# FoX: values stored by head, normalisation of a pair of heads within the next pair, GDN inverse tiles zeroed once by GpSimd; tail: sample work and SSD chunks spread among output-projection tiles

## The chip, the cores and the metric

The kernel runs on one core of a Trainium2 chip. The time is that of the device, in microseconds (us), from the first instruction to the last. Engines are named as in the profile: PE is TensorE (PEld its weight loads), DVE is VectorE, ACT is ScalarE, POOL is GpSimd, SP is SyncE, which only issues DMAs. A "q" behind the name (SPq) is the engine's sequencer, which also issues DMAs.

## The reference, cut to what matters

One layer of a hybrid model with four mixers of width 512 each, on a prompt of 1024 tokens and on 8 x 4 = 32 sample tokens. In the words of the reference:

```
proj  = x @ w_in
y_a   = rms_norm(gated_delta_rule(q, k, v, g, beta, S0)) * silu(a_gate)        # GDN, 4 heads
y_b   = rms_norm((ssd_scan(x, dt, A, B, C, h0) + D * x) * silu(b_gate)) * ssd_norm_w   # SSD, 8 heads, 2 groups
y_c   = forgetting_attention(q, k, v, cumsum(logf)) * silu(c_gate)             # FoX, 8 heads of 64
y_d   = softmax(q @ memory_k) @ memory_v * silu(d_gate)                        # memory attention
mixed = concat(y_a, y_b, y_c, y_d)                                             # 2048 wide
x_new = layer_norm(ALPHA * x + mixed @ w_out)
```

The samples have states and a paged cache of their own. Inputs and outputs are float32.

## The kernel before, in words

Work is laid out with features on the partitions. Large products run as three passes, high part times high part, high times low, low times high: `mh` is a tile rounded by ACT (L1545), `ml` is what is left of it (POOL, L1546), and the weights `wo` have both parts (ACT L1516, DVE L1517).

The stages of the profiled execution are: projections with the paged decode up to some 760 us; a change of memory pools up to 826; the **FoX stage** up to 1157; the **tail** up to 1374; the **last output group** to the end.

In the FoX stage `fox(hp)` (L545) runs four pairs of heads. For each head it loads queries and keys on the POOL queue and, once a pair, the values `vt` (L568, one buffer) and the gate `g2` on the SP queue; then for four pairs of query blocks it computes scores (`fs`, L588, with a minimum on DVE, L592), exponentials on ACT (L598), transposes (`ft`, copied to `P`) and products with the values (`fo`, L620), which DVE multiplies into `g2` (L626). After both heads it normalises: the reciprocal row sums are spread by ACT and transposed by PE (`fr`, by the helper in L219) and multiplied in by DVE (L640). Steps of `weave` alternate this with the GDN generator: `gdn_inv` (L1035) zeroes a tile `D1` (DVE, L1039) and loads diagonal blocks into it (L1041; POOL queue for the first half-head, SP for the others), `gdn_solve` inverts the chunk matrices (with `A` of L1057, masked in L1082), and `gdn_scan` runs over the chunks (`su`, `u`, L1160 to L1174). The last projections and the memory attention (`cross`) go on beside it.

In the tail, before: `out_w(12, 16)` loads weights of the output projection, two tiles of `mixed` are prepared ahead (`pre`), then in program order come the memory attention of the samples, `gdn_sample` (`xws`, `xM`), `ssd_sample` (`yi`, `yu`, `yo`), the eight SSD chunks (`ssd`, L1331) and the output groups 12 to 16, 8 to 12, 0 to 4, of eight tiles of 128 tokens each (`out`, L1549). In `out` a tile is two halves of 12 matmuls into `op` (L1574); `mixed` (L1540) loads `mr` on the SP queue (L1544) with two buffers. `out_s` gathers the 32 sample rows in `accs` (L1535). In an SSD chunk the decay `bE` is loaded, shifted and clipped by DVE (L1378, eight per chunk), exponentiated by ACT (L1380) and multiplied by `cb` on POOL (L1382); `bx` (L1350) holds the inputs, `Cz` (L1355, POOL) is a zero-padded copy of C by group, and `bb` (L1365) is the product B C. The last group, 4 to 8, is the SSD part; it starts with the sample rows (tile 8, L1576) and each tile ends with LayerNorm and its store (L1587 to L1603).

A planner (the tile framework) gives each engine its order: program order is the priority, an instruction goes when its inputs and its slot are expected ready, and `issue_after(x)` puts it behind instruction x of its engine. On the chip each engine and each DMA queue keeps that order. A tile with `bufs=n` waits for the last reader of the tile n before it.

## Time and profile before

| what | before |
| --- | --- |
| median of 3 runs (lowest, highest) | 1441.57 us (1438.98, 1443.81) |
| the profiled execution | 1434.86 us |
| its span in the trace | 1433.1 us |
| mean granted clock of TensorE | 0.976 |
| busy in the span: PE, DVE, ACT, POOL | 1329.7, 823.8, 494.7, 442.4 us |

A busy time is the sum of an engine's instructions; PEclk in a row is the granted clock as a share of full speed, 2.4 GHz, so that 0.5 is the lower of its two levels, 1.2 GHz. A wait is the idle time ahead of an instruction, with the operation whose end released it. A row `L620 ... fo<-P,vt` is the instruction at line 620, which writes `fo` from `P` and `vt`. The rows of waits have the time in all, the number of times and the longest.

### The profile page before, as it was taken

How to read it: one execution, taken by the hardware profiler on the slowest of the kernel's cores; microseconds unless marked ns; L12 is line 12 of the kernel's file. 1: busy time of each engine (PE TensorE's matmuls, PEld its weight loads, DVE VectorE, ACT ScalarE, POOL GpSimd, SP SyncE). 2: the span in 40 equal slices, each digit the busy share in tenths (PEclk: the TensorE clock that was granted, in tenths of full speed). 3: DMA queues.
4: the chain of work that ended last, by engine and by line, in shares of the span. 5: the costliest groups of instructions: out<-in, count | busy, mean ns of one | idle time of the engine just before them, and what ended most of it. 6: DMA issues, size and time to landing. Idle time of an engine off the chain costs nothing. (4 is left out here: it accounts for less than half of the span.)

```text
span 1433.1 us, 30270 instructions
## 1 busy us (share of the span) xinstructions
PE 1329.7 (93%) x11222; PEld 1110.0 (77%) x11222; DVE 823.8 (57%) x2141; ACT 494.7 (35%) x1280; POOL 442.4 (31%) x465
## 2 busy tenths in 40 slices
PE   7999999999899999999998899898988979999995
PEld 6899888888778877888887878776766756666764
DVE  4523223256576767534245655677676648856588
ACT  4422222233435343322233244454444421213232
POOL 1445322233425444432212100011111026544456
PEclk9999999999999999999999999899999999999998
DMA  6559888978778897888877834657547576655322
GB/s 246 196 169 374 331 299 323 321 269 281 240 284 306 282 307 248 303 287 323 308 259 175 239 91 118 239 147 208 137 129 252 175 234 205 198 160 121 96 67 106
DMA packets 184477, 324.30 MB, mean 226 GB/s; under 512 B 47177, under 2 KB 110954, under 8 KB 184330
## 3 DMA queue, kind: packets, MB, share of 16 engines
q1 hardware_dynamic: 113744, 241.39, 50.4%
q10 hardware_dynamic: 41930, 59.11, 11.6%
q0 software_dynamic: 28656, 21.88, 6.2%
q8 instruction: 88, 1.44, 0.4%
q14 instruction: 59, 0.48, 0.1%
HBM read 262.23 MB, written 60.01 MB: 225 GB/s over the span
## 5 line engine op out<-in xcount | busy, mean ns | idle before, releaser
L356 PE MATMUL pj<-xh,wh 128*128 128x352 f32 x1152 | 382.2, 333 | 13.1 <-ACT wh L341 5.0
L356 PE MATMUL pj<-xh,wl 128*128 128x352 f32 x1152 | 379.5, 329 | 3.3 <-DVE wl L342 3.3
L356 PE MATMUL pj<-xl,wh 128*128 128x352 f32 x1152 | 379.1, 329 | 0.0
L356 PEld LDWEIGHTS pj<-xh,wh 128*128 128x128 f32 x1152 | 219.1, 191 | 28.1 <-issue 10.7
L356 PEld LDWEIGHTS pj<-xh,wl 128*128 128x128 f32 x1152 | 219.8, 191 | 11.5 <-issue 6.3
L356 PEld LDWEIGHTS pj<-xl,wh 128*128 128x128 f32 x1152 | 219.3, 190 | 10.6 <-issue 9.9
L1574 PE MATMUL op<-wo,mh 128*128 128x512 f32 x512 | 162.9, 398 | 3.1 <-DVE lr L1587 1.6
L672 POOL DMA_INDIRECT lf<-in_logf,ix x64 | 67.9, 1062 | 203.4 <-DVE cb L675 163.4
L342 POOL TENSOR_TENSOR wl<-wr,wh 128x1024 fp32r<-128x1024 f32 x41 | 97.9, 2387 | 104.3 <-ACT wh L341 94.3
L742 DVE SCALAR_TENSOR_TENSOR Oacc<-Oacc,dmb,dO 128x512 f32<-128x512 f32 x64 | 47.5, 743 | 142.3 <-PE dO L737 134.1
L1574 PEld LDWEIGHTS op<-wo,mh 128*128 128x128 f32 x512 | 95.6, 190 | 29.6 <-issue 6.0
L1574 PE MATMUL op<-wo,ml 128*128 128x512 f32 x256 | 102.0, 401 | 5.5 <-POOL ml L1546 5.5
L917 DVE SCALAR_TENSOR_TENSOR y<-u,cw,y 128x1080 f32<-128x1080 f32 x54 | 80.1, 1484 | 21.9 <-ACT y L915 21.5
L718 PEld LDWEIGHTS dA<-pg,QD 128*32 128x32 f32 x2048 | 59.8, 109 | 39.7 <-issue 25.8
L718 PE MATMUL dA<-pg,QD 128*32 128x128 f32 x2048 | 80.6, 275 | 7.6 <-DMA pg<-in_cache 7.5
L598 ACT ACTIVATE S<-S,mn 128x512 f32<-128x512 f32 (+2 forms) x96 | 58.5, 610 | 50.8 <-DVE mn L592 24.3
L737 PE MATMUL dO<-pg,dP 128*32 128x512 f32 x512 | 71.8, 605 | 4.1 <-ACT dP L734 3.9
L726 ACT ACTIVATE dmb<-dmb 128x1 f32<-128x1 f32 x64 | 18.7, 293 | 131.6 <-DVE dmb L725 116.3
L1574 PEld LDWEIGHTS op<-wo,ml 128*128 128x128 f32 x256 | 48.4, 189 | 20.2 <-POOL ml L1546 7.1
L592 DVE CUSTOM_DVE_ANT_0 S<-fs,cB 128x512 f32<-128x512 f32 (+2 forms) x96 | 52.5, 551 | 19.9 <-PE ft L219 15.0
L1193 POOL TENSOR_TENSOR rb<-ra,constG 128x4 f32<-128x4 f32 (+1 forms) x9 | 8.7, 971 | 156.5 <-DVE ra L1192 156.5
L620 PE MATMUL fo<-P,vt 128*64 128x128 f32 x576 | 47.9, 288 | 9.6 <-DMA vt<-vD 7.7
(521 smaller groups left out, 2450.2 us busy)
## 6 DMA issues: line engine op xcount, KB each, us to landing
pg<-in_cache SPq DMA_DIRECT2D x256, 512.0 KB
wr<-in_w_in SPq DMA_DIRECT2D x48, 512.0 KB
k<-kD POOLq DMA_DIRECT2D x16, 512.0 KB, 18.2
wq<-in_w_out SPq DMA_DIRECT2D x16, 512.0 KB
mr<-mixD SPq DMA_DIRECT2D x32, 256.0 KB
xr<-in_xT SPq DMA_DIRECT2D x8, 528.0 KB
gateD<-gt ACTq DMA_DIRECT2D x24, 176.0 KB
mrow<-in_w_mem SPq DMA_DIRECT2D x8, 512.0 KB
```

The lines of the kernel that those rows point to most:

```text
L342: (eng or self.se).tensor_tensor(out=l, in0=r, in1=h.bitcast(F32), op=ALU.subtract)
L356: nc.tensor.matmul(ps[:n], lhsT=w[:, k, :], rhs=x[:, k, s], start=(k == 0 and q == 0), stop=(k == KD - 1 and q == 2))
L592: nc.vector.tensor_tensor_reduce(out=S[:, :w], in0=p[:, :w], in1=cB[:, c0:c1], op0=ALU.add, op1=ALU.min, scale=1.0, scalar=3e38, accum_out ...
L598: nc.scalar.activation(out=S[:, :w], in_=S[:, :w], func=AF.Exp, scale=-1.0, bias=mn[:, 0:1], accum_out=rs[:, qt, h2, i:i + 1])
L620: d = nc.tensor.matmul(o[64 * half:64 * half + 64, 0:128], lhsT=vt[:, kt, 64 * h2:64 * h2 + 64], rhs=P[qt, b4], start=(kt == 0), stop=(kt ...
L672: nc.gpsimd.indirect_dma_start(out=lf, out_offset=None, in_=I["logf"], in_offset=bass.IndirectOffsetOnAxis(ap=ix[:, j:j + 1].bitcast(U32), ...
L718: nc.tensor.matmul(ps[32 * b:32 * b + 32, 0:n], lhsT=QD[:, 4 * gr + b, hp, :], rhs=key(hp, b), start=(hp == 0), stop=(hp == 3), tile_posit ...
L726: nc.scalar.activation(out=mb[:, 1:2], in_=m, func=AF.Exp, scale=-1.0, bias=mb[:, 0:1])
L737: nc.tensor.matmul(po[32 * b:32 * b + 32, :], lhsT=P[:n, 32 * b:32 * b + 32], rhs=value(b), start=True, stop=True, tile_position=(0, 32 * b))
L742: nc.vector.scalar_tensor_tensor(out=O_, in0=O_, scalar=mb[:, 1:2], in1=po, op0=ALU.mult, op1=ALU.add)
L917: nc.vector.scalar_tensor_tensor(out=y, in0=u[:, i:i + CWD], scalar=w[:, i:i + 1], in1=y, op0=ALU.mult, op1=ALU.add)
L1574: nc.tensor.matmul(p[:m], lhsT=l[:, k, :], rhs=W[k][0][:, w, s], start=(k == 0 and q == 0), stop=(k == kn - 1 and q == 2))
```

## The change

In FoX, `fox_v` stores the values so that a head's half lies together, and `fox` loads a tile of half the size for each head, with two buffers. The normalisation becomes a generator, `fox_norm`; `fox` returns it, and the next pair of heads runs one half of it after the scores of each of its first two pairs of query blocks (`next(ended, None)`); the last one runs at the end. In GDN, two tiles `D1z` are zeroed once by POOL and filled in turn by `gdn_inv`; the solve writes its own `D1`.

In the tail, samples and SSD chunks become generators with more steps (in `gdn_sample` and `ssd_sample` most are bare `yield`s) that `weave` spreads among the 24 tiles of the first three output groups, and `spaced` puts the instructions of a step behind the last matmul of the tile before, `lastop`. `mixed` takes its tiles from another pool, with three buffers, and loads on the POOL queue; `pre` is gone. In an SSD chunk `Cz` goes, B C is two products of 64 rows each in two PSUM tiles; the shift and clip of the decay moves from DVE to ACT as Relu; the norm weight is no longer multiplied into `y` but into rows 4 to 8 of `w_out`. These weights get a pool of their own (`ow2`), `out_s(0)` comes after the third group, and in the last group the sample rows come second.

```diff
         vt = self.row_tile("vt")
+        vv = vt[:, :T].rearrange("p (h n c) -> p n h c", h=2, c=64)
...
-            self.copy(vt[:, 512 * a:512 * a + 512], p)
+            self.copy(vv[:, 4 * a:4 * a + 4], p.rearrange("p (n h c) -> p n h c", h=2, c=64))
...
-    def fox(self, hp):
+    def fox(self, hp, ended):
...
-        vt = fx.tile([128, 8, 128], F32, tag="vt", name="vt", bufs=1)
...
-            if h2 == 0:
-                with behind(self.gl, hd - GL):
-                    nc.sync.dma_start(vt, self.vD[hp].rearrange("p (n c) -> p n c", c=128))
+            vt = fx.tile([128, 8, 64], F32, tag="vt", name="vt", bufs=2)
+            with behind(self.gl, hd - GL):
+                nc.sync.dma_start(vt, self.vD[hp][:, 512 * h2:512 * h2 + 512].rearrange("p (n c) -> p n c", c=64))
+                if h2 == 0:
                     nc.sync.dma_start(g2, self.gateD[8 + hp])
...
                 yield
+                next(ended, None)
                 o = self.g("fo")
...
-                                d = nc.tensor.matmul(o[64 * half:64 * half + 64, 0:128], lhsT=vt[:, kt, 64 * h2:64 * h2 + 64],
+                                d = nc.tensor.matmul(o[64 * half:64 * half + 64, 0:128], lhsT=vt[:, kt, :],
...
+        return self.fox_norm(hp, g2, rs)
+
+    def fox_norm(self, hp, g2, rs):
+
+        nc, fx = self.nc, self.fx
...
+            if a == 1:
+                nc.scalar.dma_start(self.mixD[2][:, hp, :], g2)
+            yield
...
+        nc, w = self.nc, {}
 
         self.scan = self.g("su")
+
+        self.D1z = [self.ga.tile([128, 4, 32], F32, name=f"D1z{i}") for i in range(2)]
+        for t in self.D1z:
+            nc.gpsimd.memset(t, 0.0)
         self.gdn_inv(0)
         run(self.gdn_solve(0, w))
...
-        D1 = self.ga.tile([128, N, 32], F32, tag="D1", name="D1", bufs=2)
-        nc.vector.memset(D1, 0.0)
+        D1 = self.D1z[i % 2]
...
             (nc.sync if i else nc.gpsimd).dma_start(D1[16 * b:16 * b + 16, :, 16 * (b % 2):16 * (b % 2) + 16],
...
-        D1, DT1, AL, P1, P3 = self.D1[i], sm("DT1"), sm("AL"), sm("P1", 16), sm("P3")
+        D0, D1, DT1, AL, P1, P3 = self.D1[i], sm("D1"), sm("DT1"), sm("AL"), sm("P1", 16), sm("P3")
         A, DT = big("A", D["A"], eng), big("DT")
         nc.vector.memset(DT, 0.0)
         if i < 7:
...
-        nc.vector.transpose(out=fl(DT1), in_=fl(D1))
+        nc.vector.transpose(out=fl(DT1), in_=fl(D0))
...
-                nc.tensor.matmul(p[q, n * 16:(n + 1) * 16], lhsT=D1[q, n, :], rhs=P1[q, n, :], start=True, stop=True, tile_position=(32 * i, 32 * i))
+                nc.tensor.matmul(p[q, n * 16:(n + 1) * 16], lhsT=D0[q, n, :], rhs=P1[q, n, :], start=True, stop=True, tile_position=(32 * i, 32 * i))
...
 
+        yield
         p = self.g("xgb")
...
-        Cz = [sb.tile([128, 2, 128], F32, name=f"Cz{i}") for i in range(2)]
-        for c in Cz:
-            nc.gpsimd.memset(c, 0.0)
...
-            cz = Cz[n % 2]
-            for g in range(2):
-                nc.gpsimd.tensor_copy(cz[G[g], g, :], bx[G[g], 5, :])
...
-            nc.tensor.matmul(p[:, 128:384], lhsT=bx[:, 4, :], rhs=cz, start=True, stop=True)
+
+            p2 = self.g("bb")
+            for g, o in enumerate((p[:, 128:256], p2[:, 0:128])):
+                nc.tensor.matmul(o, lhsT=bx[G[g], 4, :], rhs=bx[G[g], 5, :], start=True, stop=True)
...
-            nc.vector.tensor_tensor(out=cb, in0=p[:, 128:384].rearrange("p (g i) -> p g i", g=2),
-                                    in1=self.c("mincl").unsqueeze(1).to_broadcast([128, 2, 128]), op=ALU.mult)
+            for g, o in enumerate((p[:, 128:256], p2[:, 0:128])):
+                nc.vector.tensor_tensor(out=cb[:, g, :], in0=o, in1=self.c("mincl"), op=ALU.mult)
...
             for hh in range(8):
-                nc.vector.tensor_scalar(out=E[:, hh, :], in0=E[:, hh, :], scalar1=self.gam[:, n, 4 + hh:5 + hh], scalar2=0.0,
-                                        op0=ALU.subtract, op1=ALU.min)
-            nc.scalar.activation(out=E, in_=E, func=AF.Exp)
+                nc.scalar.activation(out=E[:, hh, :], in_=E[:, hh, :], func=AF.Relu, scale=-1.0, bias=self.gam[:, n, 4 + hh:5 + hh])
+            nc.scalar.activation(out=E, in_=E, func=AF.Exp, scale=-1.0)
...
+            yield
...
+            yield
             p = self.g("bq")
             nc.tensor.matmul(p[:, 0:1], lhsT=j2, rhs=self.c("one"), start=True, stop=True)
...
-            nc.vector.tensor_tensor(out=y, in0=y, in1=_bc(self.pv[:, 91:95], 128), op=ALU.mult)
             nc.scalar.dma_start(self.mixD[1][:, :, s], y)
-            yield
...
-            hs = sb.tile([128, 2, 256], F32, tag="shs", name="shs", bufs=2)
...
-    def out_w(self, k0, k1):
+    def out_w(self, k0, k1, pool=None):
 
         nc, ow = self.nc, self.ow
         W = []
         for k in range(k0, k1):
-            w = ow.tile([128, 2, 1024], F32R, tag="wo", name="wo", bufs=self.nwo)
+            w = (pool or ow).tile([128, 2, 1024], F32R, tag="wo", name="wo", bufs=self.nwo)
             r = ow.tile([128, 1024], F32, tag="wq", name="wq", bufs=4)
             with self.tc.issue_after(self.res[min(NW, len(self.res)) - 1].ins) if self.res else nullcontext():
                 nc.sync.dma_start(r, self.I["w_out"][k])
-            nc.scalar.copy(w[:, 0, :], r)
-            nc.vector.tensor_tensor(out=w[:, 1, :], in0=r, in1=w[:, 0, :].bitcast(F32), op=ALU.subtract)
+            if k0 == 4:
+                f = self.pv[:, 87 + k:88 + k]
+                nc.scalar.activation(out=w[:, 0, :], in_=r, func=AF.Identity, scale=f)
+                nc.vector.scalar_tensor_tensor(out=w[:, 1, :], in0=r, scalar=f, in1=w[:, 0, :].bitcast(F32), op0=ALU.mult, op1=ALU.subtract)
+            else:
+                nc.scalar.copy(w[:, 0, :], r)
+                nc.vector.tensor_tensor(out=w[:, 1, :], in0=r, in1=w[:, 0, :].bitcast(F32), op=ALU.subtract)
             W.append((w, r))
...
-        raw, mh, ml = (self.ow.tile([128, kn, 128], d, tag=t, name=t, bufs=2) for t, d in (("mr", F32), ("mh", F32R), ("ml", F32R)))
-        nc.sync.dma_start(raw, self.mixD[k0 // 4][:, q0:q0 + kn, n * 128:(n + 1) * 128])
+        pool, nb, eng = self.mixp
+        raw, mh, ml = (pool.tile([128, kn, 128], d, tag=t, name=t, bufs=nb) for t, d in (("mr", F32), ("mh", F32R), ("ml", F32R)))
+        eng.dma_start(raw, self.mixD[k0 // 4][:, q0:q0 + kn, n * 128:(n + 1) * 128])
...
-    def out(self, k0, k1, W, first=False, last=False, pre=()):
...
-        for n in ((8,) if last else ()) + tuple(range(8)):
+        for n in (0, 8, 1, 2, 3, 4, 5, 6, 7) if last else range(8):
...
-                mh, ml = pre.pop(0) if pre else self.mixed(k0, k1, n)
+                mh, ml = self.mixed(k0, k1, n)
...
+                            self.lastop = nc.tensor.matmul(p[:m], lhsT=l[:, k, :], rhs=W[k][0][:, w, s], start=(k == 0 and q == 0), stop=(k == kn - 1 and q == 2))
...
             def foxes():
+                ended = iter(())
                 for hp in range(4):
-                    yield from self.fox(hp)
+                    ended = yield from self.fox(hp, ended)
+                run(ended)
...
-            pre = [self.mixed(12, 16, n) for n in range(2)]
...
+            self.mixp = self.op, 3, nc.gpsimd
             with ExitStack() as cx:
                 self.sb2 = R("ssd", cx)
                 with ExitStack() as cy:
                     self.dm = self.pool("crsm", ctx=cy)
                     self.cross_sample()
-                with ExitStack() as cy:
-                    self.ga = self.pool("gdns", ctx=cy)
-                    self.load_const("A", self.ga, nc.sync)
-                    self.gdn_sample()
-                with ExitStack() as cy:
-                    self.sb2, sb2 = self.pool("ssds", ctx=cy), self.sb2
-                    self.load_const("A", self.sb2, nc.sync)
-                    self.ssd_sample()
-                    self.sb2 = sb2
-                run(self.ssd())
-                self.out_s(12, W, first=True)
-                run(self.out(12, 16, W, first=True, pre=pre))
-                for k in KO:
-                    W = self.out_w(k, k + 4)
-                    self.out_s(k, W)
-                    run(self.out(k, k + 4, W))
+                def samples():
+                    with ExitStack() as cy:
+                        self.ga = self.pool("gdns", ctx=cy)
+                        self.load_const("A", self.ga, nc.sync)
+                        yield from self.gdn_sample()
+                    with ExitStack() as cy:
+                        self.sbs = self.pool("ssds", ctx=cy)
+                        self.load_const("A", self.sbs, nc.sync)
+                        yield from self.ssd_sample()
+
+                def spaced(gen):
+
+
+                    while True:
+                        with self.tc.issue_after(self.lastop.ins):
+                            if next(gen, self) is self:
+                                return
+                        yield
+
+                def groups():
+                    V = W
+                    self.out_s(12, V, first=True)
+                    yield from self.out(12, 16, V, first=True)
+                    for k in KO:
+                        V = self.out_w(k, k + 4)
+                        if k:
+                            self.out_s(k, V)
+                        yield from self.out(k, k + 4, V)
+                    self.out_s(0, V)
+
+                weave((groups(), 24), (spaced(samples()), NSM), (spaced(self.ssd()), 17))
+                ow2 = self.pool("outw2", ctx=cl)
+                V = self.out_w(4, 8, ow2)
             self.op2 = self.pool("outl", ctx=cl)
-            W = self.out_w(4, 8)
-            self.out_s(4, W)
-            run(self.out(4, 8, W, last=True))
...
+            self.out_s(4, V)
+            run(self.out(4, 8, V, last=True))
```

## Rows read from the trace of the kernel before

**Rows 1.** The page: length of the profiled execution.
```profile
span 1433.1 us, 30270 instructions
```

**Rows 2.** Stages: stretch, length, PE/PEld/DVE/ACT/POOL busy us (instructions), PEclk, DMA share, GB/s.
```profile
826.00:1157.00 331.00, 300.36 (x3123) 240.16 (x3126) 221.21 (x722) 151.05 (x472) 34.20 (x44) 0.96 0.56 169
1157.00:1374.00 217.00, 201.80 (x1223) 144.41 (x1215) 140.99 (x304) 52.36 (x81) 99.86 (x94) 0.98 0.56 160
1374.00:1434.00 60.00, 44.70 (x193) 35.66 (x192) 48.40 (x82) 15.58 (x22) 36.10 (x31) 0.90 0.26 90
```

**Rows 3.** Waits of PE, FoX stage: us in all, times, longest.
```profile
PE fr L219 <- DVE g L640: 6.5, 2, 5.0
...
PE su L1164 <- DVE u L1161: 2.7, 1, 2.7
```

**Rows 4.** Waits of PE, tail.
```profile
PE op L1574 <- POOL ml L1546: 5.5, 3, 2.8
PE op L1576 <- DVE accs L1535: 2.8, 1, 2.8
PE xws L1281 <- DVE xM L855: 1.8, 4, 0.6
```

**Rows 5.** Timeline around 1000 us: start, length, operation [idle before].
```profile
993.01 0.41 SPq L568 DMA_DIRECT2D vt<-vD  x1
...
1004.17 1.09 PE L620 MATMUL fo<-P,vt 128*64 128x128 f32 x6 [7.71 <-DMA vt<-vD]
```

**Rows 6.** Windows of 5 us after three stops of PE, columns as rows 2.
```profile
1005.00:1010.00 5.00, 5.00 (x21) 4.16 (x20) 2.78 (x7) 1.02 (x4) 0.00 (x0) 0.57 0.00 0
1090.00:1095.00 5.00, 5.00 (x23) 4.71 (x24) 4.67 (x13) 2.62 (x6) 2.48 (x3) 0.53 1.00 365
1300.00:1305.00 5.00, 2.22 (x6) 1.81 (x6) 0.32 (x1) 0.00 (x0) 4.08 (x6) 0.79 0.19 56
```

**Rows 7.** Timeline around 1088 us.
```profile
1086.25 1.17 DVE L1082 TENSOR_TENSOR AL<-A,constG 32x128 f32<-32x128 f32 x4 [4.07 <-DMA A<-aD3A]
...
1088.01 0.59 DVE L626 TENSOR_TENSOR g<-fo,g 64x128 f32<-64x128 f32 x2
...
1089.90 1.11 PE L219 MATMUL fr<-constG,rr 128*128 128x128 f32 x4 [5.02 <-DVE g L640]
```

**Rows 8.** Waits for the memset of L1039: SP in FoX stage, POOL before it.
```profile
SPq L1041 <- DVE D L1039: 37.2, 3, 16.5
...
POOL D L1041 <- DVE D L1039: 30.6, 1, 30.6
```

**Rows 9.** Waits of POOL and of SP, tail.
```profile
POOL Cz L1355 <- DMA bx<-bD: 43.0, 6, 9.3
...
SPq L1544 <- POOL ml L1546: 63.8, 17, 9.6
```

**Rows 10.** Timeline around 1302 us.
```profile
1300.78 0.63 POOL L1355 COPY Cz<-bx 64x128 f32<-64x128 f32 x2 [9.18 <-DMA bx<-bD]
...
1302.81 0.77 PE L1574 MATMUL op<-wo,ml 128*128 128x512 f32 x1 [2.78 <-POOL ml L1546]
```

**Rows 11.** Lines, tail: operation, count | busy us, mean ns | idle before, releasers.
```profile
L1546 POOL TENSOR_TENSOR ml<-mr,mh 128x512 fp32r<-128x512 f32 x30 | 40.7, 1358 | 41.1 <-ACT mh L1545 40.6
...
L1602 POOL TENSOR_TENSOR acc<-acc,lb 128x512 f32<-128x512 f32 x14 | 19.4, 1392 | 10.8 <-DVE acc L1601 5.6 <-DVE lr L1587 5.2
...
L1378 DVE TENSOR_SCALAR bE<-bE,gam 128x128 f32<-128x128 f32 x64 | 18.1, 344 | 10.2 <-DMA bE<-gS 5.4 <-ACT Cg L1375 4.9
...
L1367 ACT COPY bt<-bb 128x128 f32<-128x128 f32 x8 | 2.1, 263 | 14.5 <-PE bb L1365 14.5
...
L1365 PE MATMUL bb<-Cz,bx 128*128 128x256 f32 x16 | 4.8, 380 | 0.0
```

**Rows 12.** Issues of DMAs on POOL: landing of L561, durations ns of L672.
```profile
DMA to landing us min/median/max: 14.6/17.2/25.9
...
L672 POOL DMA_INDIRECT lf<-in_logf,ix x64: 942/971/1977, 104.1 to 697.0; - x64
```

More of the change, by code (lines that the diff above doesn't have):

```diff
@@ L42 @@
 KO = (8, 0)
+NSM = 26
 MARK = (0, 0, 1, 1, 2, 2, 3, 3, 4, 4)
@@ L1263, in gdn_sample @@
         nc.vector.tensor_copy(XT, p[:, 0:128])
+        yield
         p = self.g("xw")
@@ L1285, in gdn_sample @@
         u, o = sq("xu"), sq("xo")
+        yield
         p = states("xws", wk, True)
         nc.vector.tensor_tensor(out=u, in0=wv, in1=p[:, 0:128], op=ALU.subtract)
+        yield
         p = states("xo", qd, False)
@@ L1474, in ssd_sample @@
         for b2 in range(4):
-            hs = sb.tile([128, 2, 256], F32, tag="shs", name="shs", bufs=2)
+            hs = sb.tile([128, 2, 256], F32, tag="shs", name="shs", bufs=4)
             nc.sync.dma_start(hs, self.I["sst"][:, 2 * b2:2 * b2 + 2, :])
@@ L1496, in ssd_sample @@
         yf = y[R].rearrange("p h c -> p (h c)")
+        yield
         p = self.g("ygs")
@@ L1500, in ssd_sample @@
         self.ssd_finish(yf, p[:NS], NS)
+        yield
         p = self.g("yo")
@@ L1547, in mixed, with out @@
         return mh, ml
-    def out(self, k0, k1, W, first=False, last=False, pre=()):
+    def out(self, k0, k1, W, first=False, last=False):
         nc, I, O, op = self.nc, self.I, self.O, self.op
@@ L1573, in out @@
                         for q, (l, w) in enumerate(((mh, 0), (mh, 1), (ml, 0))):
-                            nc.tensor.matmul(p[:m], lhsT=l[:, k, :], rhs=W[k][0][:, w, s], start=(k == 0 and q == 0), stop=(k == kn - 1 and q == 2))
+                            self.lastop = nc.tensor.matmul(p[:m], lhsT=l[:, k, :], rhs=W[k][0][:, w, s], start=(k == 0 and q == 0), stop=(k == kn - 1 and q == 2))
                 else:
```

16 lines of the change are left out of this document (12 added, 4 removed).

## The prediction

> **What bounds the kernel now.** I read the stage windows first, then the waits of PE stage by stage, then the timeline around the longest ones. The span is 1433.1 us [rows 1]. In the FoX stage PE is busy 300.4 of 331 us, in the tail up to the last output group 201.8 of 217 us, and in the last group 44.7 of 60 us, 24 matmuls (a tile) taking 44.70 / 193 x 24 = 5.6 us [rows 2]. No other engine comes near: DVE has 221 of 331 and 141 of 217 us, POOL 100 of 217 us [rows 2]. So PE's work sets the time, and an edit is worth what PE stands still for, plus what the lower clock costs after each stop. The whole possible gain is some 30 us of idle time in FoX and 15 us in the tail; I go through what ends it.
>
> In FoX, beside the stop for the value tile `vt` (part A), PE waits 6.5 us in two stops for the normalisation (`fr` behind DVE's L640), and 2.7 us for a DVE result of the GDN scan (L1161) [rows 3]. In the tail it waits 5.5 us for POOL's `ml`, 2.8 us for `accs` at the switch to the last group, and 1.8 us for `xM` of the GDN samples [rows 4].
>
> **The change, part by part.** The sum is made against the profiled execution, 1434.9 us (span 1433.1, 1.8 around it), 6.7 us under the median of the runs, 1441.6; I add 6.7 at the end.
>
> A. *Values by head.* `vt` has one buffer for a pair of heads, so its load is issued only at 993.01, after the last `fo` of the pair before, and PE stands 7.71 us until 1004.17 [rows 5]. With a half tile per head and two buffers, the slot of head 0 is free half a pair earlier, and the load runs under the other head's work. After the stop PE restarts at 1.2 GHz: the granted clock of 1005 to 1010 us is 0.57, so 86% of it, 4.3 us, ran at half speed, which cost 2.15 us [rows 6]. Together -9.9 us. At the least half of that: PE's next inputs come from the same DVE and ACT queues. Eight loads in place of four cost SP four more issues of about 0.4 us [rows 5], which hide under its idle time. I take -9.9.
>
> B. *Normalisation within the next pair.* The 5.02 us stop is the second `fr`, which waits for L640 on DVE, and DVE itself stood 4.07 us for the DMA of `A` until 1086.25 and then ran L1082 for 1.17 us [rows 7]. Taking `fr` out of PE's way does not bring `A` earlier: what PE has next needs DVE too, and DVE's first result for it would be `g` of L626, from 1088.01 on for 0.59 us [rows 7]. So PE goes on at about 1088.6 in place of 1089.9: -1.3 us, and the clock that follows (0.53 in 1090 to 1095, so 4.7 us at half speed, 2.35 us lost [rows 6]) shortens by a third: -2 us in all. Bounds: 0 and -5.0 - 2.35 = -7.4. The last pair has no next pair and keeps its norm: its `fr` stop, the other part of the 6.5 us, stays.
>
> C. *Inverse tiles zeroed once by GpSimd.* Eight DVE memsets of `D1` go. What matters is SP: its loads of `D` waited 37.2 us in three stretches for that memset [rows 8], and the loads of `A`, `vt` and gates stand behind them in SP's queue. DVE's L1082 waits for `A`, and I read the 2.7 us stop of PE [rows 3] as that wait seen from PE. I take half: -1.5 us (0 to -2.7). On the other side, at the start of the GDN stage POOL waited 30.6 us for this memset [rows 8]; the two memsets now stand in POOL's own queue, and if they come ahead of FoX's first loads, FoX starts later. Projection tiles cover PE at that time. I take +1 us; without the cover it would be some 6.
>
> D. *No zero-padded `Cz`, output loads on the POOL queue.* This is the tail's main fault. POOL's copies into `Cz` wait 43.0 us in six stretches for `bx` [rows 9], and `ml`, which PE needs, stands behind them on POOL: at 1300.78 `Cz` starts after 9.18 us of waiting, and PE starts at 1302.81 after 2.78 us [rows 10]. The circle closes on SP, whose `mr` loads (L1544) wait 63.8 us for POOL's `ml` to free their slot [rows 9] with `bx` queued behind them. The change cuts it at both ends: `Cz` is gone, `mr` leaves SP and gets a third buffer. The 5.5 us go [rows 4], and the slow stretch after 1300 (clock 0.79, so 2.1 us at half speed, 1.05 us [rows 6]): -6.6 us; at the least half, as `ml` still stands behind other POOL work.
>
> E. *Own pool for the last group's weights, out_s(0) late, samples' rows second.* The weights of rows 4 to 8 no longer wait for slots of the group before, and PE starts the last group with tile 0 and not with `accs`: -2.8 us [rows 4], 0 at the least. The norm weight folded into them and the DVE pass over `by` that goes are off PE's path.
>
> F. *Chunk products with 64 rows.* `bb` has 16 passes of 256 columns [rows 11]; eight pairs become 32 passes of 128 columns, on two halves of the array. The time of a pass is not shown free of its latency; if halves overlap it saves at most half of 380 ns a pair, 1.5 us; if not, nothing. I take -0.8.
>
> G. *Spreading.* `spaced` only orders PE: a step's matmuls stand behind the last matmul of the output tile before, so DVE and ACT have a tile's time to prepare them. Of the 1.8 us for `xM` I take -1 (0 to -1.8).
>
> H. *Start of the tail.* The two output tiles loaded ahead (`pre`) are gone. The new `mr` lies in a pool that takes FoX's memory, and sample matmuls may not go ahead of tile 0, so PE may stand until `mr` lands and POOL has made `ml` (1.36 us [rows 11]). Below: nothing, if that memory is free before FoX ends. Above: 17.2 us, the median of POOL-issued loads from issue to landing [rows 12], so 18.6. Those loads are twice the size and went out four at a time while DMAs were busy, so I stay nearer zero: +5 us.
>
> I. *Who carries the new work.* ACT takes 64 Relu of 128x128 from DVE: 64 x 263 ns [rows 11] = 17 us on an engine with 52 of 217 us [rows 2]; DVE gives up 18.1 us [rows 11]. Zero, since neither is the bound. POOL gets 32 DMA issues: at 971 ns each [rows 12] 31 us on top of 136 us in a tail of 277 [rows 2]. Queued behind them are `ml`, the decay products that PE's `by` waits for, and the final additions. In the last group a tile costs POOL 1.36 + 2 x 1.39 + 0.97 = 5.1 us [rows 11, 12] against PE's 5.6: it fits, barely, and only for the five tiles not loaded ahead. Zero, with the bound in the rivals.
>
> That bound has a page. The rows show issues of 971 ns with the longest at 1977 [rows 12]. The Trainium skill's page "SBUF — State Buffer" says in the box on DVE blocking DMA (section "SBUF: two separate sides") that the descriptors of a DMA issued from GpSimd are written through the port pair that it shares with VectorE, and that the SP or ACT queue is the better place, which speaks against this change; its section "A bandwidth-pool intuition that's wrong (but worth ruling out)" gives about 3.1 us in place of 0.62 beside a VectorE copy. An estimate by that page: 32 x 2.5 = 80 us more on POOL. The trace agrees only in part: its longest issue is under 2 us.
>
> Sum: -9.9 - 2 - 1.5 + 1 - 6.6 - 2.8 - 0.8 - 1 + 5 = -18.6 us; 1434.9 - 18.6 = 1416.3, and with 6.7 us the median comes to **1423 us**.
>
> **Rivals.**
> *More comes back.* All gains at their upper bound and no stop at the tail's start: -9.9 - 7.4 - 2.7 - 6.6 - 2.8 - 1.5 - 1.8 = -32.7, 1409 us. For it: the SP queue is freed in both stages. Against: DVE's waits for `A` stay. 0.10.
> *A new wait takes the place.* A and D give half (-5, -3.3), the tail starts 5 us later, the rest nothing: -3.3, 1438 us. For it: the whole order of instructions is made anew, and PE has dozens of small stops. Against: the stops removed are single, long and have one cause each. 0.17.
> *POOL held by DVE.* Each issue takes 1.98 us [rows 12]: the last group's tiles cost POOL 6.1 us, 0.5 over PE, five times, and the first load comes 1 us later: about +4, 1427 us. 0.08.
> *Slower: late loads on the POOL queue.* With three buffers a tile can come once in a third of (landing + `ml`). At 20.5 us to landing, within the 14.6 to 25.9 seen [rows 12], that is 21.9 / 3 = 7.3 us against 5.6: +13.9 us over eight tiles, and +21.9 at the tail's start: -23.6 + 21.9 + 13.9 = +12.2, 1454 us. It decides from some 18.5 us to landing, where +4 remains. Against: a load of half the size, alone. 0.10.
>
> **How the numbers follow.** The forecast has 0.55. About 0.3% is what a measurement of this kernel tells from no change (1437.2 to 1445.9). Faster: 0.55 + 0.10 + 0.08 + a third of the new-wait case, 0.06 = 0.79; within: 0.11; slower: 0.10. The range leaves out the slower case, the upper end of the new-wait case and the lower part of the first rival: 1407 to 1441.
>
> **What would show it.** A: no wait of `fo` for `vt`, and a clock of 1.0 there. B: the `fr` stop gone, but DVE still waiting for `A`. C: SP with no wait for a memset. D: no PE wait for `ml` above 1 us, and SP's wait at L1544 gone. E: the switch to the last group without a stop. H: a stop of PE between FoX's last matmul and the first `op`, about 5 us. The prediction is wrong if that stop is above 15 us, if POOL becomes the engine that PE waits for in the last group, or if new stops in FoX add up to the 13 us that A to C take away.

## The result, and the profile after

The change makes the kernel slower: 1480.71 us (1475.27 to 1484.23, 4 runs) against 1440.28 us of before (1431.33 to 1443.81), a ratio of 1.0283 with an interval of 1.0234 to 1.0331. I had forecast 1423 us. The profiled execution took 1478.13 us, its span is 1476.4 us and the mean granted clock 0.962 in place of 0.976.

The stage windows of the changed kernel, its stages cut where they end now (columns as rows 2):

```profile
826.00:1177.00 351.00, 309.39 (x3049) 246.92 (x3051) 213.05 (x695) 148.17 (x464) 32.88 (x42) 0.92 0.55 158
1177.00:1400.00 223.00, 208.04 (x1225) 149.14 (x1221) 123.80 (x251) 70.06 (x151) 111.76 (x107) 0.95 0.52 149
1400.00:1477.00 77.00, 57.93 (x228) 37.87 (x224) 57.04 (x91) 19.95 (x26) 38.73 (x34) 0.89 0.26 94
```

In FoX PE stands still for 42 us where it had 31 [rows 2], and the clock in it fell from 0.96 to 0.92; the last group stretches over 77 us where it had 60. The waits of PE in the FoX stage (us in all, times, longest):

```profile
PE ft L220 <- ACT P L215: 8.1, 3, 7.0
PE zs L877 <- DMA cmk<-in_cmk: 6.7, 2, 4.1
PE su L1178 <- DVE u L1175: 4.6, 1, 4.6
PE cT L220 <- ACT P L837: 4.2, 2, 3.7
```

and in the tail:

```profile
PE bt L220 <- DMA bx<-bD: 6.0, 1, 6.0
PE op L1606 <- DVE wo L1548: 5.4, 1, 5.4
PE op L1562 <- DMA wq<-in_w_out: 3.8, 1, 3.8
PE op L1606 <- ACT mh L1577: 2.8, 2, 1.5
PE op L1606 <- POOL ml L1578: 0.8, 2, 0.6
```

The waits that I had read are gone: none for `vt`, 0.8 us in place of 5.5 for `ml`, none for `xM`, and the switch to the last group no longer waits for `accs` [rows 3, 4]. Others stand in their place, in FoX longer ones. To compare kernels I cut each trace at three ends: of the last matmul into `dot` (the end of the decode), into `fr` (the end of FoX) and into `op`. In us:

| kernel | dot | FoX: dot to fr | tail: fr to op | behind | span |
| --- | --- | --- | --- | --- | --- |
| before | 805.4 | 350.5 | 264.4 | 12.8 | 1433.1 |
| changed | 802.9 | 373.9 | 284.9 | 14.7 | 1476.4 |

So FoX lost 23.4 us, the tail 20.5, the end 1.9, and the decode gave back 2.5: 43.3 in all. The waits explain little of the tail's part. Its two windows, cut at these ends, first of before and then of the changed kernel (columns as rows 2):

```profile
1155.90:1420.30 264.40, 247.58 (x1423) 180.48 (x1422) 181.50 (x377) 66.42 (x101) 130.31 (x120) 0.99 0.50 146
```

```profile
1176.80:1461.70 284.90, 266.17 (x1449) 187.13 (x1449) 170.01 (x324) 88.11 (x174) 143.99 (x135) 0.95 0.46 136
```

PE stands still for 1.9 us more and is busy for 18.6 us more, at a clock of 0.95 in place of 0.99: the lower clock is at most some 12 us of that (an estimate: 5% of 284.9 us less 1% of 264.4). Of the rest, 2.8 us are traced below (part F); what is left stays open.

The experiments take the two halves apart.

### The profile page after: what moved, and what is told of

The parts are those of the page before. It is cut to its first block, busy times and chain, and to the rows that moved or that the text cites. A ratio compares the mean times of both kernels' runs of the same rounds, so it can differ in the third digit from the quotient of the medians.

```text
span 1476.4 us, 30264 instructions
## 1 busy us (share of the span) xinstructions
PE 1355.9 (92%) x11238; PEld 1121.7 (76%) x11238; DVE 809.5 (55%) x2069; ACT 513.9 (35%) x1344; POOL 456.0 (31%) x481
## 5 line engine op out<-in xcount | busy, mean ns | idle before, releaser
L1606 PE MATMUL op<-wo,mh 128*128 128x512 f32 x512 | 168.8, 410 | 8.2 <-DVE wo L1548 5.4
L1578 POOL TENSOR_TENSOR ml<-mr,mh 128x512 fp32r<-128x512 f32 x32 | 42.1, 1318 | 107.2 <-ACT mh L1577 107.2
L566 POOL DMA_DIRECT2D k<-kD x16 | 13.2, 828 | 184.8 <-PE fs L595 150.4
L1612 DVE SCALAR_TENSOR_TENSOR acc<-acc,op 128x512 f32<-128x512 f32 x48 | 32.8, 684 | 55.0 <-PE op L1606 54.8
```

What stands on the lines that cost most here:

```text
L1578: nc.gpsimd.tensor_tensor(out=ml, in0=raw, in1=mh.bitcast(F32), op=ALU.subtract)
L1606: self.lastop = nc.tensor.matmul(p[:m], lhsT=l[:, k, :], rhs=W[k][0][:, w, s], start=(k == 0 and q == 0), stop=(k == kn - 1 and q == 2))
L1612: nc.vector.scalar_tensor_tensor(out=acc[:, s], in0=acc[:, s], scalar=ALPHA if first or n == 8 else 1.0, in1=p[:m], op0=ALU.mult, op1=ALU.add)
```

## The experiments

Ratios are to the kernel before, with their intervals. Stage lengths (FoX, tail) are cut as above, from the one profiled execution of each; before has 350.5 and 264.4.

**The two halves, each alone.** `fox_only`: 1485.07 us, 1.0312 (1.0267 to 1.0358).

It is the kernel before with the change's lines in `fox_v`, `fox`, `fox_norm`, `foxes`, `gdn`, `gdn_inv` and `gdn_solve`, of which the core is:

```diff
-        vt = fx.tile([128, 8, 128], F32, tag="vt", name="vt", bufs=1)
+            vt = fx.tile([128, 8, 64], F32, tag="vt", name="vt", bufs=2)
...
+                next(ended, None)
...
+        self.D1z = [self.ga.tile([128, 4, 32], F32, name=f"D1z{i}") for i in range(2)]
```

> The kernel before with the FoX and GDN parts of the change alone (values by head, normalisation in the next pair, two tiles zeroed once by POOL); the tail is the old one. Theory that the two halves add up: in the trace of the changed kernel the last fr of FoX ends at 1176.8 us in place of 1155.9, so this kernel is some 21 us slower than before, 1461 us. Rival, that the FoX end is late only because the new tail keeps sample matmuls and the first output tiles from filling its stops: then the old tail fills them and half or more of it goes, 1440 to 1450 us. Rival, that FoX is no worse and all comes from the tail: 1440 us or less.

`tail_only`: 1464.23 us, 1.0139 (1.0086 to 1.0193).

It is the kernel before with all other lines of the change, of which the core is:

```diff
-        nc.sync.dma_start(raw, self.mixD[k0 // 4][:, q0:q0 + kn, n * 128:(n + 1) * 128])
+        eng.dma_start(raw, self.mixD[k0 // 4][:, q0:q0 + kn, n * 128:(n + 1) * 128])
...
+                weave((groups(), 24), (spaced(samples()), NSM), (spaced(self.ssd()), 17))
+                ow2 = self.pool("outw2", ctx=cl)
```

> The kernel before with the tail's parts of the change alone; FoX and GDN are the old ones. If the halves add up: from the end of FoX to the end of the third output group the changed kernel took 11.6 us more, from there to the last matmul 8.9 more, and 1.9 more behind it, so 22 us slower than before, 1462 us. Rival, that the tail loses only because FoX ends late and alone: the same as before, 1440 us, or faster by the stops at ml that are gone (5 us).

Each half alone is slower, and they don't add up: 45 + 24 us alone, 40 together. `tail_only` came out as expected (tail 288.5 us, FoX 350.3). `fox_only` lost in FoX as expected, and more (378.4), but the old tail, which it has unchanged, lost 19 us too (283.5). No theory of mine foresaw that.

**The GDN part alone.** `gdn_zero_only`: 1489.03 us, 1.0314 (1.0268 to 1.0361).

```diff
+        self.D1z = [self.ga.tile([128, 4, 32], F32, name=f"D1z{i}") for i in range(2)]
+        for t in self.D1z:
+            nc.gpsimd.memset(t, 0.0)
...
-        D1 = self.ga.tile([128, N, 32], F32, tag="D1", name="D1", bufs=2)
-        nc.vector.memset(D1, 0.0)
+        D1 = self.D1z[i % 2]
```

> The kernel before with one part alone: the two GDN inverse tiles zeroed once by POOL. Theory: POOL's memsets and the loads of D behind them now go ahead of FoX's first loads in POOL's queue, GDN's first solve goes first (lp at 821 in place of 845 us in the changed kernel) and FoX starts 10 us later (first fs at 830 in place of 820), and as FoX is the last to end, the stage ends at least those 10 us later: 1450 to 1460 us. Rival, that the late FoX comes of the values by head or of the normalisation within the next pair: 1440 us here.

This part, the cheapest of my sum, costs 48 us by itself, as much as the whole change (the intervals overlap), and far more than the 10 to 20 us that I expected here. POOL's timeline, first of the kernel before and then of `gdn_zero_only`, shows what the memsets do at the start:

```profile
770.50 0.54 POOL L1057 DMA_DIRECT2D Kp<-aD0Kp  x1
771.03 0.86 POOL L561 DMA_DIRECT2D q<-qD  x1
...
807.61 1.06 POOL L1041 DMA_DIRECT2D D<-dX  x2 [30.56 <-DVE D L1039]
```

```profile
769.34 0.46 POOL L1024 MEMSET D1z<- 128x128 f32 x2
...
774.03 4.07 POOL L1044 DMA_DIRECT2D D1z<-dX  x8
779.17 0.83 POOL L561 DMA_DIRECT2D q<-qD  x1 [1.07 <-PE pj L356]
```

Before, the loads of `D` stood behind FoX's first loads and waited there for DVE; now they are issued by 778 us. The planner gives PE another order: the first solve comes ahead of the first scores. The matmuls into `lp` (solve) and `fs` (scores), by tile (durations ns min/median/max, first and last start), of before:

```profile
L1086 PE MATMUL lp<-DT,AL x256: 177/178/198, 844.5 to 1098.5; 32*32 32x16 f32 x128
```

```profile
L588 PE MATMUL fs<-k,q x96: 279/474/988, 819.9 to 1138.1; 128*128 128x512 f32 x48, 128*128 128x256 f32 x32, 128*128 128x384 f32 x16
```

and of `gdn_zero_only`:

```profile
L1089 PE MATMUL lp<-DT,AL x256: 177/178/198, 827.7 to 1103.1; 32*32 32x16 f32 x128
```

```profile
L588 PE MATMUL fs<-k,q x96: 280/441/775, 839.8 to 1174.0; 128*128 128x512 f32 x48, 128*128 128x256 f32 x32, 128*128 128x384 f32 x16
```

GDN's solve starts 17 us earlier, FoX 20 us later, and FoX's last scores come 36 us later: the order of the whole stage is made anew from there. In the new order the stops have another cause. From the timeline of `gdn_zero_only`:

```profile
948.48 0.33 ACTq L641 DMA_DIRECT2D mixD<-g  x1
948.85 0.21 ACT L1090 COPY P<-lp 128x64 f32<-128x64 f32 x1 [10.73 <-DMA QK<-aD1QK]
949.12 0.63 PE L1095 MATMUL lt<-P,D1z 32*32 32x16 f32 x32 [9.38 <-ACT P L1090]
...
1114.22 2.13 SPq L1547 DMA_DIRECT2D mr<-mixD  x2
...
1126.85 0.62 ACT L1548 CAST mh<-mr 128x512 fp32r<-128x512 f32 x1 [14.11 <-DMA mr<-mixD]
...
1128.29 1.01 PE L1142 MATMUL wv<-Vp,DT 128*128 128x128 f32 x3 [11.47 <-ACT DT L1133]
```

The copy at 948.85 does not read `QK`. Ahead of it in ACT's order stood the store `mixD<-g` (L641), and that went out at 948.48, when the load of `QK`, which SP had issued at 925.2, had landed: in the trace both DMAs count on the same semaphore. ACT stood 10.7 us, and PE 9.4 behind it. At 1113 us ACT came to the rounding of an output tile whose load went out only at 1114 and stood 14.1 us for it. All that FoX and GDN needed of ACT stood behind in its order, and PE stood 11.5 us.

**Who zeroes.** `gdn_zero_by_dve`: 1439.03 us, 0.9997 (0.9958 to 1.0036). `after_zero_by_dve`, the same in the changed kernel: 1457.79 us, 1.0124 (1.0054 to 1.0195).

```diff
-            nc.gpsimd.memset(t, 0.0)
+            nc.vector.memset(t, 0.0)
```

> As gdn_zero_only (before, with two inverse tiles zeroed once), but DVE zeroes them and not POOL. In the built order the first loads of D then stand behind FoX's first q and k in POOL's queue again, and the first scores (fs) ahead of the first solve (lp) on PE, as in the kernel before; the loads of D have no memset ahead of them in either. Theory that the place of POOL's memsets and loads costs the 48 us: the time of before or up to 5 us less, 1435 to 1443 us, with the last fr some 350 us after the last projection of the decode (dot), not 381. Rival, that tiles that are zeroed only once cost it (loads that now wait for PE's lt, an order of SP's loads of another kind): 1470 us or more.

> The changed kernel with the two tiles zeroed by DVE and not by POOL. FoX then goes first as in the kernel before. The changed kernel against tail_only says that the FoX and GDN parts cost 17 us in it: if all of that is POOL's memsets, 1464 us; if the values by head and the normalisation then bring their 12 us too, 1452 us. Rival, that the order of the start doesn't matter under the new tail: 1481 us.

One word takes the 48 us away. `gdn_zero_by_dve` has the order of before at the start and its stages (FoX 350.9, tail 263.7). In the changed kernel it gives 23 us, between the two times that I expected, and FoX is then 340.5 us, 10 us shorter than before. Zeroing once by itself is worth nothing that these runs can tell (0.9997, so at most 6 us either way).

**One memset on POOL.** `first_memset_by_pool`: 1468.18 us, 1.0212 (1.0159 to 1.0265).

```diff
-        nc.vector.memset(D1, 0.0)
+        (nc.vector if i else nc.gpsimd).memset(D1, 0.0)
```

> The kernel before with one word changed: of the eight memsets of D1 the first one alone, that of half-head 0, is on POOL; the tile keeps its two rotating buffers. Theory that the 48 us of gdn_zero_only come only of what the start's memset on POOL does to the order (the first loads of D ahead of FoX's q and k on POOL, the first solve ahead of the first scores on PE): 1480 to 1490 us. Rival, that zeroing only once has a part in it: half of that, 1460 us, or less.

Between the two: 31 of the 48 us come of the first memset alone, with FoX at 385.1 us, 4 us longer than in `gdn_zero_only` (381.3). That one was slower by 11 us in the tail of its profiled execution (283.0 against 272.1) and by 9 in the decode, which no edit here touches; why the tail is longer with tiles that are zeroed once, under this order of the start, stays open.

**The sample rows of the third group.** `rows_before_third`: 1466.63 us, 1.0180 (1.0137 to 1.0223), 14 us less than the changed kernel.

```diff
-                        if k:
-                            self.out_s(k, V)
+                        self.out_s(k, V)
                         yield from self.out(k, k + 4, V)
-                    self.out_s(0, V)
```

> The changed kernel with one thing moved: the sample rows' products of the third output group (out_s(0)) stand ahead of its tiles again and not behind them. Theory: they read the tiles wq, whose slots the loads of the last group's weights need; in the changed kernel SP stands 56.5 us for them at L1541 and issues the four loads at 1401.8 us, after the last tile of the third group, so the last group starts 8.7 us after it and its first half tile takes 9.5 us in place of 2.9. With the rows early the loads go out early, and the 9 us that the switch had lost come back: 1472 us. Rival, that the weights' scaling on ACT and DVE sets the switch: 1481 us as the changed kernel.

The wait in the queue of SP, tail, and the timeline at the switch, of the changed kernel:

```profile
SPq L1541 <- PE op L1562: 58.2, 2, 56.5
```

```profile
1401.84 1.92 SPq L1541 DMA_DIRECT2D wq<-in_w_out  x4
...
1405.54 3.17 PE L1562 MATMUL op<-wq,ms 128*32 128x512 f32 x4 [3.75 <-DMA wq<-in_w_out]
...
1408.64 0.80 PE L1606 MATMUL op<-wo,mh 128*128 128x512 f32 x1
```

and the same loads in `rows_before_third`:

```profile
1337.74 1.09 SPq L1541 DMA_DIRECT2D wq<-in_w_out  x2
...
1341.09 2.09 SPq L1541 DMA_DIRECT2D wq<-in_w_out  x2
```

The loads go out 60 us earlier, the switch has no stop, and the tail is 272.1 us in place of 284.9. The theory held; the gain was 14 and not 9 us. The low clock behind the stop (0.88 from 1402 to 1416 us in the changed kernel) is 1.7 us of that, by an estimate; and in the profiled execution FoX is 6 us shorter too (367.8), far from the lines moved. The rest of the difference I have not traced.

**DVE held off by POOL.** `rows_state_on_dve`: 1459.79 us, 1.0113 (1.0051 to 1.0175), 7 us less than `rows_before_third`.

```diff
-            nc.gpsimd.tensor_tensor(out=St[h], in0=St[h], in1=_bc(self.cdS[:, :, h], 128), op=ALU.mult)
+            nc.vector.tensor_tensor(out=St[h], in0=St[h], in1=_bc(self.cdS[:, :, h], 128), op=ALU.mult)
```

> rows_before_third with one thing changed: the four products of the GDN samples' state with its decay (xS, L1316) run on DVE and not on POOL. In the trace of rows_before_third one DVE instruction, the low part of a weight tile (wo, L1548), lasts 10.5 us in place of 1.2, over just the time in which POOL runs these four and two more products back to back, and PE stands 5.35 us for it at 1260 us. Theory that DVE is held off by POOL's products of two operands: DVE's wo takes 1.2 us again, the stop at 1260 goes, with 3 us of low clock behind it, and the four products cost DVE some 5 us beside other work: 1459 to 1462 us against 1466.6. Rival, that the long entry is a wait for ACT's high part or for a slot: wo is as late as before, 1467 us.

The timeline of `rows_before_third`:

```profile
1251.79 1.22 DVE L1548 TENSOR_TENSOR wo<-wq,wo 128x1024 fp32r<-128x1024 f32 x1
1253.53 12.13 DVE L1548 TENSOR_TENSOR wo<-wq,wo 128x1024 fp32r<-128x1024 f32 x2
1255.26 7.52 POOL L1316 TENSOR_TENSOR xS<-xS,cdS 128x1024 f32<-128x1024 f32 x4
1262.75 0.61 POOL L1426 TENSOR_TENSOR hst<-hst,hcd 128x256 f32<-128x256 f32 x1
1263.32 1.25 POOL L1397 TENSOR_TENSOR Cg<-Cg,bx 128x512 f32<-128x512 f32 x1
...
1265.71 0.79 PE L1606 MATMUL op<-wo,mh 128*128 128x512 f32 x1 [5.35 <-DVE wo L1548]
```

and the lines of `wo` (busy us, mean ns, idle before), first of `rows_before_third`, then of `rows_state_on_dve`:

```profile
L1548 DVE TENSOR_TENSOR wo<-wq,wo 128x1024 fp32r<-128x1024 f32 x8 | 19.9, 2503 | 1.2 <-ACT wo L1547 1.2
```

```profile
L1548 DVE TENSOR_TENSOR wo<-wq,wo 128x1024 fp32r<-128x1024 f32 x8 | 12.0, 1513 | 1.1 <-ACT wo L1547 1.1
```

The second of the pair took 10.5 us, from 1255.16 on, and ended 1.1 us, about its own length, behind POOL's sixth product in a row; the same entry of 10.5 us, with the same 1.1 us, stands in the traces of the changed kernel, `tail_only` and `after_zero_by_dve`. With `xS` on DVE it is 1.2 us and the 5.35 us stop is gone.

**All three together.** `combined` (`after_zero_by_dve` + `rows_before_third` + `rows_state_on_dve`): 1440.61 us, 1.0020 (0.9985 to 1.0054).

> The changed kernel with three things put right at once: the two tiles zeroed by DVE, the sample rows of the third group ahead of its tiles, xS of the GDN samples on DVE. If the three gains add up (23, 14 and 7 us off 1481): 1437 us, the time of before. Rival, that they overlap, as the order is made anew by each: 1445 to 1455 us.

The three gains add up (23 + 14 + 7 = 44; measured 40), and with that the kernel is where it was before the change. FoX has 344.8 us, 6 less than before, the tail 273.4, 9 more.

**The start of the tail.** `combined_chunks_later`: 1436.68 us, 0.9991 (0.9968 to 1.0013). `combined_decay_later`: 1438.95 us, 1.0005 (0.9973 to 1.0037).

```diff
+            if n == 0:
+                yield
+                yield
             p = self.g("bt")
...
-                weave((groups(), 24), (spaced(samples()), NSM), (spaced(self.ssd()), 17))
+                weave((groups(), 24), (spaced(samples()), NSM), (spaced(self.ssd()), 19))
```

> As combined, and the products of the first SSD chunk stand two output tiles behind its loads. In the trace of after_zero_by_dve PE stands 7.4 us at 1155 us for bx, whose load goes out only when FoX's memory is free, and the clock is at its lower level for the 13.7 us from 1156.8 on. Two tiles are 11 us of work, so the stop goes, and most of the low clock: 7.4 us and some 3 us less than combined, 1427 us. Rival, that the start of the tail is short of other inputs too (mr, mh): 3 us less at most, 1434 us.

```diff
-        nc.scalar.copy(mh, raw)
+        self.lastmh = nc.scalar.copy(mh, raw)
...
+                with self.tc.issue_after(self.lastmh.ins) if n == 0 else nullcontext():
+                    nc.scalar.activation(out=E[:, hh, :], in_=E[:, hh, :], func=AF.Relu, scale=-1.0, ...)
```

> As combined_chunks_later, and on ACT the eight Relu of the first SSD chunk's decay stand behind the rounding (mh) of the third output tile. In the trace of combined_chunks_later the stop for bx has only moved: PE stands 8.1 us at 1166 us for mh, as ACT keeps its order and waits with the Relu for bE, a load issued together with bx. Theory that this one queue position holds the start of the tail: the stop goes and most of the 13.6 us of low clock there, 8 + 4 us: 1425 us against 1436.7. Rival, that the next input (the chunk's own work two tiles later, or mr) is just as late: 1433 us or more.

The rival held in both: the stop only moves. The timelines, of `combined_chunks_later` and of `combined_decay_later`:

```profile
1170.00 2.44 ACT L1402 ACTIVATE bE<-bE,gam 128x128 f32<-128x128 f32 x8 [12.75 <-DMA bE<-gS]
...
1174.09 2.08 PE L1609 MATMUL op<-wo,mh 128*128 128x512 f32 x4 [8.14 <-ACT mh L1580]
```

```profile
1173.25 1.28 ACT L1399 ACTIVATE Cg<-bE 64x512 f32<-64x512 f32 x2 [12.41 <-DMA bE<-gS]
...
1178.17 0.29 DVE L1258 TENSOR_TENSOR xE<-xE,constA 128x128 f32<-128x128 f32 x1 [11.95 <-ACT xE L1255]
...
1179.28 0.45 PE L220 MATMUL xat<-constG,xA 128*128 128x128 f32 x1 [13.35 <-DVE xA L1266]
```

First PE waited for `bx`; then ACT stood 12.75 us for the decay of the first chunk and PE for `mh` behind it; then ACT stood 12.41 us for that of the second chunk and PE for the samples' `xA`. What is late is a group of loads that went out only once FoX had ended, and whichever engine comes to one of them first stops what is behind it. The second chunk's `bE` went out 10 us later still (1157.5 us, against 1147.5 for the first, in `combined_decay_later`), with four loads of `acc` ahead of it in SP's queue that took 6.7 us to issue.

**Values and normalisation.** `values_norm_only`: 1449.55 us, 1.0031 (0.9978 to 1.0085). `values_only`: 1439.42 us, 1.0014 (0.9976 to 1.0052). `norm_only`: 1457.19 us, 1.0104 (1.0067 to 1.0141). `combined_no_values_norm`: 1447.82 us, 1.0051 (1.0015 to 1.0087).

The first edit is that of `values_only`, the second that of `norm_only`; `values_norm_only` has both, `combined_no_values_norm` is `combined_chunks_later` without either.

```diff
-            self.copy(vt[:, 512 * a:512 * a + 512], p)
+            self.copy(vv[:, 4 * a:4 * a + 4], p.rearrange("p (n h c) -> p n h c", h=2, c=64))
...
-        vt = fx.tile([128, 8, 128], F32, tag="vt", name="vt", bufs=1)
+            vt = fx.tile([128, 8, 64], F32, tag="vt", name="vt", bufs=2)
```

```diff
+                next(ended, None)
...
-                    yield from self.fox(hp)
+                    ended = yield from self.fox(hp, ended)
+                run(ended)
```

> The kernel before with the values by head and the normalisation within the next pair, without the GDN part. My prediction for these two was -12 us: the 7.7 us stop for vt and the 5.0 us stop for fr go. Theory that only the GDN part is harmful: 1425 to 1432 us. Rival, that FoX's new steps meet new stops of the same length: 1440 us; added to gdn_zero_only they gave -4 us.

> The kernel before with the values by head alone. My step A said -9.9 us, 1428 to 1431 us, by the stop for vt that goes. values_norm_only measured no gain with both; if the normalisation is what spoils it, this one is at 1430 us; if every shift in FoX costs the old tail as much, at 1438 to 1450 us with a FoX stage that is shorter by 6 us or more.

> The kernel before with the normalisation within the next pair alone. My step B said -2 us (0 to -7.4), 1430 to 1438 us. If it is what spoils values_norm_only: 1445 to 1455 us. The 7.7 us stop for vt should still be there.

> combined_chunks_later with the values by head and the normalisation within the next pair undone. If these two are worth in the whole what they gave to the FoX stage alone (from the last projection of the decode to the last fr 342.5 us in values_norm_only against 350.5 before): 8 us more than combined_chunks_later, 1445 us. Rival, that nothing of it reaches the end: 1437 us.

| kernel | FoX | tail |
| --- | --- | --- |
| before | 350.5 | 264.4 |
| values_only | 345.3 | 269.1 |
| norm_only | 354.7 | 284.7 |
| values_norm_only | 342.5 | 281.8 |
| combined_chunks_later | 341.8 | 268.8 |
| combined_no_values_norm | 350.7 | 270.1 |

Values by head shorten FoX by 5 us, both together by 8, and the old tail, of which no line has changed, gives back 5, 20 and 17 us. The 5 us of `values_only` rest on one execution each; the 20 of `norm_only` are borne out by its median, 18 us above that of before. Under the new tail both are worth 11 us by the medians (1447.8 against 1436.7) or 9 by the ratios, and 9 in FoX. In one window each (columns as rows 2), the tail of before and that of `norm_only`:

```profile
1156.00:1421.00 265.00, 247.50 (x1422) 180.40 (x1422) 182.10 (x377) 66.42 (x101) 131.01 (x121) 0.99 0.50 146
```

```profile
1161.00:1446.00 285.00, 258.05 (x1418) 187.92 (x1410) 183.77 (x374) 66.26 (x101) 125.13 (x121) 0.94 0.44 135
```

The same work, with 27 us in which PE stands still in place of 17 and a clock of 0.94 in place of 0.99. Its waits of PE:

```profile
PE op L1581 <- POOL ml L1553: 7.7, 3, 3.9
PE yi L1485 <- DMA shs<-in_sst: 4.5, 1, 4.5
PE bt L219 <- DMA bx<-bD: 2.7, 1, 2.7
```

The wait for `shs`, a load of the samples' state on SP, is in `values_only` and `values_norm_only` too (4.7 and 4.4 us) and not in the kernel before. I take it that the old tail had little slack, its loads standing in SP's queue in an order that fits one FoX; that is an argument, and no run tests it. Which of FoX's instructions upsets the tail I have not found out.

## Why the prediction was wrong

The measured time is 57.7 us above the forecast. The step that failed most is C, where I priced an edit at the start of FoX as a delay and not as a new order. Next come E, which overlooked what holds the tiles `wq`, and G, which left out that POOL's products can hold DVE off. The three edits of `combined` answer these three and take 40 us back. The other 17.6 us are gains that did not come: in the trace of `combined` FoX is 5.7 us shorter than before where A to C had 12.4, and the tail is 9.0 us longer where D to H had 6.2 less. An 8.0 us stop for `bx` in that tail belongs to H; the rest stays open.

**A, values by head (-9.9).** The mechanism was right: no stop for `vt`, FoX 5.2 us shorter alone, and with B 8 us, or 9 to 11 in the whole under the new tail, against -11.9 for A and B. What failed is that I added it up as if the tail would follow unchanged; in `values_only` nothing of it arrives at the end.

**B, normalisation (-2).** The `fr` stop shrank from 6.5 [rows 3] to 0.8 us, and DVE still waits for `A`, as foreseen. Alone it makes FoX 4.2 us longer, with the stop for `vt` (7.0 us) still in it, and the tail 20 longer: outside its bounds of 0 to -7.4, by an effect far from the instructions that it moves.

**C, zeroing by POOL (-1.5 + 1).** The step that failed most. I had seen that the memsets stand ahead of FoX's first loads in POOL's queue, and priced that as a delay, of 1 us with cover and 6 without. Its price is not the delay but the order: it was 48 us alone, 23 in the changed kernel. The 30.6 us that POOL waited for DVE's memset [rows 8] looked like a loss; but in every kernel with that wait FoX goes first, and `gdn_zero_by_dve`, where it is 32.6 us, is as fast as before. And SP's 37.2 us for the memset [rows 8] were worth nothing that can be told from no change: they are gone in `gdn_zero_by_dve`, and the time is the same.

**D, `Cz` and the output loads (-6.6).** The 5.5 us for `ml` became 0.8, and SP's wait for `ml` is gone. Whether the whole -6.6 came, no run shows by itself; the tail as a whole is longer.

**E, the last group (-2.8).** Wrong in sign, by one of its three edits. I followed the slots of `wo`, which the new pool makes free, and not those of `wq`, from which the weights are made and which the late `out_s(0)` holds to the end of the third group. The late `out_s(0)` cost 14 us.

**F (-0.8).** The 32 passes of `bb` take 7.6 us in the changed kernel, against 4.8 [rows 11]: +2.8 us of PE's busy time. One pair of before, and the first two chunks of the changed kernel:

```profile
1172.56 0.60 PE L1365 MATMUL bb<-Cz,bx 128*128 128x256 f32 x2
```

```profile
1195.96 0.80 PE L1386 MATMUL bb<-bx 64*128 64x128 f32 x4
...
1223.12 0.49 PE L1386 MATMUL bb<-bx 64*128 64x128 f32 x2
...
1228.09 0.48 PE L1386 MATMUL bb<-bx 64*128 64x128 f32 x2
```

In the first chunk the four passes stand together, and those of the two halves start 7 ns apart: they overlap. They took 0.80 us at 1.2 GHz, so 0.40 at full clock (an estimate), less than the 0.60 of before. In the other seven chunks the second product comes 1.1 to 5.0 us behind the first, with other work between them, and each takes some 0.49 us by itself. So the saving was there, and the order did not let it come.

**G (-1).** The waits for `xM` are gone, as foreseen. What the sum had at nothing is where the spreading puts the samples' work: POOL's four `xS` products came to stand beside DVE's work on the weights, DVE was held off, and PE stood 5.4 us for `wo`. In `rows_state_on_dve` that was worth 7 us.

**H (+5).** The stop is there, but for the chunk's `bx` (6.0 us), and with a clock of 1.2 GHz for the 10 us from 1191 on; the two moves that I tried only shifted it.

**I (0).** POOL's issues cost less than I had put: 747 to 818 ns, median 787, for the 32 of `mr`, and POOL did not become the bound. The price of about 3.1 us beside a VectorE copy that the Trainium skill's page "SBUF — State Buffer" gives (section "A bandwidth-pool intuition that's wrong (but worth ruling out)") is not seen in these 32 issues. What did happen is the other direction of that exclusion: in its section "SBUF: two separate sides" that page of the Trainium skill says that a VectorE operation with two inputs in SBUF and a GpSimd operation that reads SBUF exclude each other, the first to start holding the ports for its whole instruction. The trace agrees that the two exclude each other, but not on who goes first: by its record DVE started 0.1 us ahead of POOL's first product (1255.16 against 1255.26), and it was held for six POOL instructions in a row, 10.5 us.

My rivals had the right kind of case, a new wait in place of the old one with the order made anew, at 1438 us and 0.17. Its price was a guess from my own gains; in FoX the stops that came were longer than those that went, and the lower clock came with them (54 us of it in place of 27). The sign I got wrong because the one rival on the slow side was late loads on POOL's queue, which the runs don't show: in the changed kernel the `mr` loads landed 3.2 to 12.3 us after their issue, 4.6 in the median.

No version clearly beats the kernel before: `combined_chunks_later` is level with it.

## What to carry to other kernels

Where a planner fixes the order of each engine, an edit that changes when a thing seems ready can change the order of all that follows: before pricing a wait that goes, ask what that wait had put behind what, above all at the start of a stage. For every buffer that an edit frees, follow the tiles that feed it (`wq` behind `wo`) to their last reader. And try the parts alone: the smallest one can carry the whole loss.

## What the runs showed of the hardware

- A DVE operation on two SBUF operands (`wo`, L1548) was held off for as long as POOL ran products back to back: 10.5 us in place of 1.2, over six POOL instructions, in four traces of kernels with this tail order; it was 1.2 us again in `rows_state_on_dve`, where POOL did not run four of them.
- ACT stood 12.4 to 14.1 us at a time for a load, with PE waiting 8.1 to 13.4 us for ACT's work behind it; and once 10.7 us for a store in its queue that was issued only when another engine's load had landed.
- Products of 64 rows on the two halves of the array overlapped when they stood together (starts 7 ns apart), and not when other work stood between them.
- With more stops came more of the lower clock: in its FoX stage `gdn_zero_only` has 56 us without PE where before has 33, and a clock of 1.2 GHz for 58 us where before has 27.
- The decode ahead of all this ended between 800.1 and 816.1 us in the seventeen profiled executions, though none of the experiments touches it but for the order in which values are stored; runs of the kernel before spread from 1425 to 1452 us. So the stages are compared by their lengths and the totals by medians, not by single spans.
